# A transformer block on one NeuronCore: weight splits and background products placed differently at the attention entry and ahead of three norms

## The chip, the cores and the metric

The kernel runs on one core of a Trainium2 chip. The metric is the device time of one execution in microseconds (us), lower is better. Engines are named as the profile names them: PE is the matrix engine (PEld its weight loads), DVE the vector engine, ACT the scalar engine, POOL GpSimd, SP the engine that issues most DMAs.

## What is computed

One sequence of 256 tokens with 1024 channels goes through two blocks. The first has two layers, each a token mixer and a gated feed-forward net (FFN); the second is a state-space and pooling block with a mixture of experts. Each layer starts from an RMS norm whose result is scaled and shifted by vectors that come from a conditioning input (adaLN).

```python
def first_block(...):
    for i in range(DEPTH):
        mod = (silu_c @ ada_w[i] + ada_b[i])[:, None, :]
        sh1, sc1, g1, sh2, sc2, g2 = jnp.split(mod, N_MOD, axis=-1)
        h = modulate(rmsnorm(x, norm1_g[i]), sh1, sc1)
...
        if mixer == 0:
            yc, y = diff_attention(h, hc, ...)
        elif mixer == 1:
            yc, y = short_conv(h, hc, ...)
...
        x = x + g1 * y
        x = x + g2 * swiglu(modulate(rmsnorm(x, norm2_g[i]), sh2, sc2), ffn_w_in[i], ffn_w_out[i])
def second_block(...):
        u = modulate_2(rmsnorm_2(h, norm_mix_g[l]), sh1, sc1)
        proj = u @ w_in[l]
```

So the chain of stages is: attention, FFN 0, short convolution, FFN 1, the input product of the second block and its branches, experts.

## The kernel before

**Products.** Tokens lie along the free axis (T = 256), channels along the 128 partitions, so a 1024-channel activation is 8 tiles. A product in 32-bit precision is made of three matmuls (`mm3`, lines 280 to 282): high weight part by high activation, high by low, low by high. One output tile of 128 channels with 8 input tiles is therefore 24 matmuls.

**Weights.** A `Stream` brings them in 1 MB tiles (ring of 4). A unit is half a tile, 8 blocks of 128x128, so with 1024 input channels one output takes one unit. Each unit is split just ahead of its use: ACT copies the high part (`wh`, line 146), DVE subtracts to get the low part (`wl`, line 134), into a ring of 5 units. `take(n, ahead)` hands out blocks and first splits up to `ahead` units beyond the one taken; `more(n)` only splits. Both engines work strictly in the order in which the instructions were issued, so a split that is issued ahead of other work is done ahead of it.

**Background.** With each new unit, `take` also issues a share (`bg_pace`) of the adaLN sums: one weight tile by the conditioning row on DVE (`ada`, line 395), 128 in all. `hold` stops them.

**Attention.** A loop over the value products (4 steps) runs heads' scores and exponentials for the first three head halves; then a loop over 18 steps does, per step, on PE a transpose of the probabilities (`turn_p`, tile tp, copied to pT by ACT at line 801), the next scores (tile s), and the product with the values (`attend`, line 809, tile o); on DVE the maxima of the scores (line 722) and the difference of the two softmaxes (lines 737, 738); on ACT the exponentials (line 728).

**Residual.** `residual` (called after attention, after each FFN and after the convolution) makes the 8 output tiles (ps_r, or the first of them together: ps_wo, ps_so), adds each to x on DVE (line 910), squares it on ACT for the norm's mean square (`sumsq_step`, line 338) and, ahead of the three norms of class `Raw`, also splits the raw x into u (lines 930, 931).

**Norms ahead of which products run.** `Raw` covers the waiting time of a norm: the first products of the next stage are made from the un-normed u and are multiplied by the norm's rows later (`lift`). `Raw.run` does this with 3 outputs at the convolution's entry (raw1: ps_cu, ps_cu, ps_b), 4 at FFN 1 (raw3: ps_f) and 4 at the second block (raw2: ps_ssd, beside some small dt products). In it come in turn: one input tile's products of all outputs, the mean square on PE (ms, line 351), its inverse root on DVE (rs_v to rs_r), more products, the rows on PE (line 953), a copy of them (rows_s, line 956), the remaining products, and the norm itself: DVE scales x (na, line 379), ACT shifts it to hh (line 380), DVE makes the low part hl (line 383). After that all products use hh and hl. FFN 0's entry has the plain form, without products ahead (line 363).

Of the kernel before, what the change touches and what calls it, by code (L numbers as in the profile page):

```python
# [8 lines left out]
F32 = mybir.dt.float32  # L9
# [8 lines left out]
P = 128  # L18
T = 256
D = 1024  # L20
KD = 8
# [86 lines left out]
class Stream:  # L108
# [51 lines left out]
    def more(self, n, defer=False):  # L160

        self.fill(self.pos // 8 // 2 + self.ring)
        self.split_to(self.pos // 8 + n, defer)
# [74 lines left out]
class Builder:  # L238
# [93 lines left out]
    def sumsq_step(self, ms, xk, k, tag="rp_a", **kw):  # L332

        nc = self.nc
        sq = self.wk.tile([P, T], F32, tag=tag if k == 0 else "sq", name="sq", bufs=2)
        if k == 0:
            self.acc[tag] = sq
        nc.scalar.activation(sq, xk, AF.Square, **kw)  # L338
        if 0 < k < KD - 2:
            nc.gpsimd.tensor_tensor(self.acc[tag], self.acc[tag], sq, op=ALU.add)  # L340
        if k == KD - 2:
            self.acc[tag, 1] = sq
        if k == KD - 1:
            self.totals.append((ms, (self.acc[tag], self.acc[tag, 1], sq)))
# [80 lines left out]
def build(ctx, tc, ap):  # L425
    b = Builder(ctx, tc, ap)
# [319 lines left out]
    for n in range(4):  # L746
        pss = [b.ps.tile([P, 2, T], F32, tag="ps", name="ps_v") for _ in range(2)]
# [23 lines left out]
    b.bg_pace = 0.0  # L771
# [72 lines left out]
    for s in range(18):  # L844
# [6 lines left out]
        if s + 3 < 16:  # L851
            scores(s + 3)
        if s >= 4 and s % 2 == 0:
            head_turn((s - 4) // 2)
# [17 lines left out]
        if s < 13:  # L872
            st.ahead_splits()
        if s == 13:
            st.more(4)
# [10 lines left out]
    def residual(ktiles, xh, xl, gate, sums, done=(), raw=None):  # L886
# [10 lines left out]
        for n in range(KD):  # L897
            if n < len(done):
                ps = done[n]
            else:  # L900
                b.hold = raw is not None and n == KD - 1
# [6 lines left out]
                if raw and n == KD - 1:  # L908
                    st.more(4)
# [6 lines left out]
    class Raw:  # L916
# [16 lines left out]
        def steps(self, outs, more):  # L933
            w = st.take(KD * len(outs), 0)
            for k in range(KD):
                if more:
                    more(k)
                for i, o in enumerate(outs):
                    b.mm3(o[:, :T + 2], w[i * KD + k], self.H[:, k], self.L[:, k], k == 0, k == KD - 1)
                yield  # L940

        def run(self, rstd, outs, more=None):

            go = self.steps(outs, more)
            next(go)
            b.total()
            r = self.r = rstd()
            st.more(5 - len(outs))
            next(go)
            next(go)  # L950
# [180 lines left out]
    pss = [b.ps.tile([P, 2, T], F32, tag="ps", name="ps_so") for _ in range(2)]  # L1131
    so_out = together([pss[i // 2][:, i % 2] for i in range(4)], rH, rL)
# [1180 lines left out]
```

## Time and profile before

| | us |
|---|---|
| median of 3 runs | 1561.92 |
| lowest and highest run | 1558.98, 1562.48 |
| the profiled execution | 1554.01 |
| its span from first to last instruction | 1552.2 |
| PE busy | 1480.8 (95%) |
| DVE busy | 987.8 (64%) |
| ACT busy | 669.0 (43%) |
| PE clock over the span, share of full | 0.988 |

The profiled execution is 7.9 us shorter than the median. Times inside the trace count from the start of the span. Stages lie there as follows: attention's 18 steps from 155 to 217, FFN 0 from 236, the convolution's entry at 431, FFN 1's entry at 524, the second block's entry at 724, the experts from about 1000 on. A row with a bracket tells how long its engine was idle before and what ended that.

### The profile page before, as it was taken

The page shows a single profiled execution, that of the slowest core. Times are in us where ns is not written, and L with a number is a line of the kernel's source. Part 1 is how long each engine was busy: PE and PEld are TensorE (multiplying, and loading weights), DVE is VectorE, ACT ScalarE, POOL GpSimd, SP SyncE. Part 2 cuts the span into 40 slices and gives each one's busy share as a digit, 9 for nine tenths or more (in the row PEclk, how much of TensorE's full clock was granted, in tenths as well). Part 3 has the DMA queues.
Part 4 walks back from the last instruction along what each step waited for, and adds up shares of the span by engine and source line. Part 5 has one row for each costly group of instructions (what it writes and reads, how often), then busy time and mean ns, then how long its engine had stood idle before and what let it go on. Part 6 is the DMA issues. An engine that isn't in the chain of part 4 may idle for free. (4 is left out here: it accounts for less than half of the span.)

```text
span 1552.2 us, 28284 instructions
## 1 busy us (share of the span) xinstructions
PE 1480.8 (95%) x11184; PEld 1185.0 (76%) x11184; DVE 987.8 (64%) x1850; ACT 669.0 (43%) x1175; POOL 276.2 (18%) x439
## 2 busy tenths in 40 slices
PE   6999888999999999999899999999999999999996
PEld 5788578999999899999899998999634444444432
DVE  3698767888888789887888877465423333323332
ACT  3524554544455454454677765443322222222222
POOL 0170560000100100021067667001100000000000
PEclk9999999999999899999999999999999999999998
DMA  9678224987957569786444544667489999999995
GB/s 388 224 247 284 103 73 186 347 326 292 352 197 250 191 231 355 297 312 236 145 167 153 190 164 154 237 249 324 164 310 414 420 419 421 420 419 420 421 420 210
DMA packets 71429, 431.93 MB, mean 278 GB/s; under 512 B 8176, under 2 KB 8688, under 8 KB 28416
## 3 DMA queue, kind: packets, MB, share of 16 engines
q1 hardware_dynamic: 68656, 422.77, 71.0%
q0 software_dynamic: 1344, 4.80, 0.8%
q10 hardware_dynamic: 1296, 2.55, 0.5%
q8 instruction: 88, 1.44, 0.4%
q14 instruction: 45, 0.37, 0.1%
HBM read 429.01 MB, written 1.08 MB: 277 GB/s over the span
## 5 line engine op out<-in xcount | busy, mean ns | idle before, releaser
L134 DVE TENSOR_TENSOR wl<-st,wh 128x1024 fp32r<-128x1024 f32 x294 | 364.7, 1249 | 74.5 <-ACT wh L146 74.0
L146 ACT ACTIVATE wh<-st 128x1024 fp32r<-128x1024 f32 x294 | 306.2, 1055 | 113.2 <-PE ps_r L281 45.2
L280 PE MATMUL ps_f<-hh,wh 128*128 128x256 f32 x672 | 189.6, 282 | 2.5 <-ACT hh L380 2.1
L282 PE MATMUL ps_f<-hh,wl 128*128 128x256 f32 x672 | 189.5, 282 | 0.7 <-DVE wl L134 0.7
L281 PE MATMUL ps_f<-hl,wh 128*128 128x256 f32 x672 | 189.4, 282 | 0.1
L395 DVE SCALAR_TENSOR_TENSOR ada<-ada,crow 128x1024 f32<-128x1024 f32 x128 | 164.8, 1295 | 18.3 <-DMA ada<-in_ada 18.3
L340 POOL TENSOR_TENSOR sq<-sq 128x256 f32<-128x256 f32 x30 | 40.5, 1356 | 575.6 <-ACT sq L338 575.2
L280 PEld LDWEIGHTS ps_f<-hh,wh 128*128 128x128 f32 x672 | 127.6, 190 | 2.9 <-ACT hh L380 2.3
L282 PEld LDWEIGHTS ps_f<-hh,wl 128*128 128x128 f32 x672 | 127.5, 190 | 1.0 <-DVE wl L134 1.0
L281 PEld LDWEIGHTS ps_f<-hl,wh 128*128 128x128 f32 x672 | 127.6, 190 | 0.3 <-DVE hl L383 0.3
L280 PE MATMUL ps_ssd<-hh,wh 128*128 128x256 f32 x352 | 101.4, 288 | 0.0
L280 PE MATMUL ps_r<-gH,wh 128*128 128x256 f32 x352 | 98.7, 280 | 0.0
L281 PE MATMUL ps_r<-gL,wh 128*128 128x256 f32 x352 | 98.7, 280 | 0.0
L282 PE MATMUL ps_r<-gH,wl 128*128 128x256 f32 x352 | 98.7, 280 | 0.0
L282 PE MATMUL ps_ssd<-hh,wl 128*128 128x256 f32 x352 | 98.6, 280 | 0.0
L281 PE MATMUL ps_ssd<-hl,wh 128*128 128x256 f32 x352 | 98.6, 280 | 0.0
L1817 DVE TENSOR_SCALAR xb<-gtp,A,mod 128x256 f32<-128x256 f32 (+2 forms) x52 | 27.4, 526 | 111.5 <-ACT xb L1815 111.3
L1815 ACT ACTIVATE xb<-gtp,mod,A 128x256 f32<-128x256 f32 (+2 forms) x52 | 28.6, 551 | 118.6 <-PE gtp L1835 118.4
L1805 POOL TENSOR_TENSOR WG<-G,pwq 128x256 f32<-128x256 f32 (+2 forms) x24 | 14.1, 608 | 366.4 <-DVE G L1801 366.4
L274 ACT ACTIVATE oH<-wr 128x512 fp32r<-128x512 f32 (+2 forms) x53 | 33.4, 630 | 95.2 <-DVE wr L2093 82.6
L1835 PEld LDWEIGHTS gtp<-G,utH 128*128 128x128 f32 x208 | 39.2, 189 | 45.9 <-DVE xb L1817 19.7
L280 PEld LDWEIGHTS ps_ssd<-hh,wh 128*128 128x128 f32 x352 | 66.3, 188 | 1.0 <-issue 1.0
(616 smaller groups left out, 4156.0 us busy)
## 6 DMA issues: line engine op xcount, KB each, us to landing
st<-in_ws SPq DMA_DIRECT2D x151, 1024.0 KB, 6.0
ada<-in_ada SPq DMA_DIRECT2D x128, 512.0 KB, 5.0
w<-in_we SPq DMA_DIRECT2D x40, 1024.0 KB, 19.8
w_st<-in_we SPq DMA_DIRECT2D x40, 1024.0 KB, 19.8
w_y<-in_we SPq DMA_DIRECT2D x32, 1024.0 KB, 19.8
w_ut<-in_we SPq DMA_DIRECT2D x30, 1024.0 KB, 19.8
w_h<-in_we SPq DMA_DIRECT2D x21, 1024.0 KB, 19.8
x<-in_we SPq DMA_DIRECT2D x10, 1024.0 KB, 19.8
```

What stands on the lines that cost most here:

```text
L134: self.b.nc.vector.tensor_tensor(lo.rearrange("p a c -> p (a c)"), w, h.rearrange("p a c -> p (a c)"), op=ALU.subtract)
L146: nc.scalar.activation(h.rearrange("p a c -> p (a c)"), w, AF.Copy)
L274: self.nc.scalar.activation(h, src, AF.Copy)
L280: nc.tensor.matmul(out, lhsT=h[:, k], rhs=xh, start=start, stop=False, skip_group_check=True)
L281: nc.tensor.matmul(out, lhsT=h[:, k], rhs=xl, start=False, stop=False, skip_group_check=True)
L282: nc.tensor.matmul(out, lhsT=lo[:, k], rhs=xh, start=False, stop=stop, skip_group_check=True)
L340: nc.gpsimd.tensor_tensor(self.acc[tag], self.acc[tag], sq, op=ALU.add)
L395: self.nc.vector.scalar_tensor_tensor(junk, w, 1.0, crow, op0=ALU.mult, op1=ALU.mult, accum_out=dst[:, j:j + 1])
L1805: nc.gpsimd.tensor_tensor(cut(WG, tt), cut(G, tt), ws_[:, tt][:, :, None].to_broadcast([P, n, c]), op=ALU.mult)
L1815: nc.scalar.activation(out[:, k, :n], tp[:, i, :n], AF.Identity, scale=A, bias=B)
L1817: nc.vector.tensor_scalar(out[:, k, :n], tp[:, i, :n], A, B, op0=ALU.mult, op1=ALU.add)
L1835: nc.tensor.matmul(tp[:, i, :n], lhsT=hl_[:, tt, k * P:(k + 1) * P], rhs=G[:, tt, :n], start=(i == 0 and tt == 0 and hl_ is utH), stop=(tt ...
```

## The change

Five edits. The square of the last but one tile goes into another ring (`na`, 3 buffers), so that the last one finds a buffer. The adaLN sums stop one step earlier in the value loop. The two units of the output weights that were split at steps 13 and 14 of the attention loop are split at steps 0 and 2. In `residual`, the hold of the adaLN sums begins at the fifth output instead of the last after the convolution, and the split of units at the last output is gone. In `Raw`, the outputs are no longer made all together but the first two together and each other by itself, the mean square comes after three input tiles, the rows after all eight; the units of later outputs are taken, with up to three further units split, when their turn comes. The convolution's output product makes 2 instead of 4 outputs together.

```diff
 def sumsq_step(self, ms, xk, k, tag="rp_a", **kw):
-        sq = self.wk.tile([P, T], F32, tag=tag if k == 0 else "sq", name="sq", bufs=2)
+        kept = k == KD - 2
+        sq = self.wk.tile([P, T], F32, tag="na" if kept else "sq" if k else tag, name="sq", bufs=3 if kept else 2)
...
     for n in range(4):
+        if n == 3:
+            b.bg_pace = 0.0
...
-    b.bg_pace = 0.0
...
+        if s in (0, 2):
+            st.more(4 + s // 2)
...
-        if s < 13:
-            st.ahead_splits()
-        if s == 13:
-            st.more(4)
+        if 2 < s < 14:
+            st.more(5)
...
-                b.hold = raw is not None and n == KD - 1
+                b.hold = raw is not None and n >= (KD - 1 if ktiles > KD else 4)
...
-                if raw and n == KD - 1:
-                    st.more(4)
...
         def steps(self, outs, more):
-            w = st.take(KD * len(outs), 0)
-            for k in range(KD):
-                if more:
-                    more(k)
-                for i, o in enumerate(outs):
-                    b.mm3(o[:, :T + 2], w[i * KD + k], self.H[:, k], self.L[:, k], k == 0, k == KD - 1)
-                yield
+            for g in (outs[:2], *[[o] for o in outs[2:]]):
+                w = st.take(KD * len(g), 4 - len(g))
+                for k in range(KD):
+                    if more and g[0] is outs[0]:
+                        more(k)
+                    for i, o in enumerate(g):
+                        b.mm3(o[:, :T + 2], w[i * KD + k], self.H[:, k], self.L[:, k], k == 0, k == KD - 1)
+                    yield
...
-            next(go)
+            for _ in range(3):
+                next(go)
             b.total()
             r = self.r = rstd()
-            st.more(5 - len(outs))
-            next(go)
-            next(go)
+            for _ in range(KD - 3):
+                next(go)
...
-    pss = [b.ps.tile([P, 2, T], F32, tag="ps", name="ps_so") for _ in range(2)]
-    so_out = together([pss[i // 2][:, i % 2] for i in range(4)], rH, rL)
+    pss = [b.ps.tile([P, 2, T], F32, tag="ps", name="ps_so")]
+    so_out = together([pss[0][:, i] for i in range(2)], rH, rL)
```

Three places show what this moves. On DVE at the start of the attention loop, before: wl is a low weight part, ada an adaLN sum, smx the maxima of the scores of the fourth head half.

```order
L134 TENSOR_TENSOR wl<-st,wh 128x1024
L395 SCALAR_TENSOR_TENSOR ada_553,mod_92<-ada_553,crow 128x1024
L395 SCALAR_TENSOR_TENSOR ada_554,mod_92<-ada_554,crow 128x1024
L134 TENSOR_TENSOR wl<-st,wh 128x1024
L395 SCALAR_TENSOR_TENSOR ada_552,mod_92<-ada_552,crow 128x1024
L395 SCALAR_TENSOR_TENSOR ada_553,mod_92<-ada_553,crow 128x1024
L400 TENSOR_TENSOR mod_92<-mod_92,vecs 128x8
L722 TENSOR_REDUCE smx<-s 128x1 x2
L732 RECIPROCAL smx<-smx 128x2
```

The same place on DVE in the changed kernel:

```order
L134 TENSOR_TENSOR wl<-st,wh 128x1024 x2
L723 TENSOR_REDUCE smx<-s 128x1 x2
L134 TENSOR_TENSOR wl<-st,wh 128x1024
L733 RECIPROCAL smx<-smx 128x2
L738 TENSOR_SCALAR smx<-smx,lam 128x1
```

Four sums and an addition have left the queue ahead of the maxima, and one split of the output weights has come in behind them.

On ACT at the convolution's entry (raw1), before: rows_s is the copy of the norm's rows, hh the norm's result.

```order
L338 ACTIVATE sq<-x 128x256
L930 ACTIVATE u<-x,A_1_96 128x256
L146 ACTIVATE wh<-st 128x1024
L956 ACTIVATE rows_s<-rows 128x256
L380 ACTIVATE hh<-na,mod_93 128x256 x8
L146 ACTIVATE wh<-st 128x1024 x2
```

The same place on ACT in the changed kernel:

```order
L339 ACTIVATE sq<-x 128x256
L930 ACTIVATE u<-x,A_1_96 128x256
L146 ACTIVATE wh<-st 128x1024
L958 ACTIVATE rows_s<-rows 128x256
L146 ACTIVATE wh<-st 128x1024 x2
L381 ACTIVATE hh<-na,mod_93 128x256 x8
```

Two splits have moved from behind the norm's eight tiles to ahead of them. At raw3 and raw2 it is three.

On DVE at the same entry, before: rs_r is the last step of the inverse root, na and hl the two steps of the norm.

```order
L321 SCALAR_TENSOR_TENSOR rs_r<-rs_t,rs_r 128x1 x2
L134 TENSOR_TENSOR wl<-st,wh 128x1024
L379 SCALAR_TENSOR_TENSOR na<-x,A_1_96,rows_s 128x256 x3
L383 SCALAR_TENSOR_TENSOR hl<-na,mod_93,hh 128x256
L379 SCALAR_TENSOR_TENSOR na<-x,A_1_96,rows_s 128x256
```

The same place on DVE in the changed kernel:

```order
L321 SCALAR_TENSOR_TENSOR rs_r<-rs_t,rs_r 128x1 x2
L134 TENSOR_TENSOR wl<-st,wh 128x1024 x2
L380 SCALAR_TENSOR_TENSOR na<-x,A_1_96,rows_s 128x256 x3
L384 SCALAR_TENSOR_TENSOR hl<-na,mod_93,hh 128x256
L380 SCALAR_TENSOR_TENSOR na<-x,A_1_96,rows_s 128x256
```

The one split that stood there has moved ahead of the inverse root, and the two of ACT's list stand in its place, each behind its wh.

## Rows read from the trace of the kernel before

**Rows 1.** PE waits over the whole span: engine, line, releaser, total, times, longest us.

```profile
PE o L809 <- ACT pT L801: 9.0, 6, 4.0
...
PE ps_f L282 <- DVE wl L134: 3.9, 4, 1.8
```

**Rows 2.** Timeline of DVE at attention's entry: start us, duration us, instruction, idle before.

```profile
159.42 1.23 DVE L395 SCALAR_TENSOR_TENSOR ada<-ada,crow 128x1024 f32<-128x1024 f32 x1 [0.40 <-DMA ada<-in_ada]
...
160.77 1.28 DVE L722 TENSOR_REDUCE smx<-s 128x1 f32<-128x512 f32 x2
```

**Rows 3.** Timelines of ACT (second row) and PE over attention's first steps.

```profile
155.74 1.13 PE L719 MATMUL s<-kT,qT 64*128 64x512 f32 x4
...
161.49 0.69 ACT L728 ACTIVATE se<-s,smx 128x512 f32<-128x512 f32 x1 [4.99 <-DVE smx L722]
...
163.48 0.79 PE L809 MATMUL o<-v,pT 128*128 128x128 f32 x2 [4.03 <-ACT pT L801]
...
168.34 0.58 PE L809 MATMUL o<-v,pT 128*128 128x128 f32 x1
...
177.94 0.49 PE L809 MATMUL o<-v,pT 128*128 128x128 f32 x2 [0.79 <-ACT pT L801]
```

**Rows 4.** Costliest groups of the page: count | busy us, mean ns | idle before.

```profile
L134 DVE TENSOR_TENSOR wl<-st,wh 128x1024 fp32r<-128x1024 f32 x294 | 364.7, 1249 | 74.5 <-ACT wh L146 74.0
L146 ACT ACTIVATE wh<-st 128x1024 fp32r<-128x1024 f32 x294 | 306.2, 1055 | 113.2 <-PE ps_r L281 45.2
```

**Rows 5.** Timeline of DVE at FFN 0's entry.

```profile
236.27 1.22 DVE L395 SCALAR_TENSOR_TENSOR ada<-ada,crow 128x1024 f32<-128x1024 f32 x1
...
237.63 0.16 DVE L289 TENSOR_SCALAR rs_v<-ms 128x4 f32<-128x4 f32 x1
```

**Rows 6.** Timeline of PE at raw1: its first raw product, the last of the first output with hh.

```profile
430.71 0.28 PE L280 MATMUL ps_cu<-u,wh 128*128 128x258 f32 x1
...
443.83 0.28 PE L282 MATMUL ps_cu<-hh,wl 128*128 128x256 f32 x1
```

**Rows 7.** Timelines of PE, ACT and DVE around raw1's norm, and ACT's two splits.

```profile
435.29 0.39 PE L953 MATMUL rows<-csts,rs_r 128*128 128x128 f32 x2
...
435.94 0.38 ACT L956 ACTIVATE rows_s<-rows 128x256 f32<-128x256 f32 x1 [2.68 <-PE rows L953]
...
436.36 1.28 DVE L379 SCALAR_TENSOR_TENSOR na<-x,A,rows_s 128x256 f32<-128x256 f32 x3 [0.38 <-ACT rows_s L956]
...
442.13 1.27 DVE L383 SCALAR_TENSOR_TENSOR hl<-na,mod,hh 128x256 fp32r<-128x256 f32 x3
...
442.67 2.00 ACT L146 ACTIVATE wh<-st 128x1024 fp32r<-128x1024 f32 x2
```

**Rows 8.** Timelines of DVE (second row) and PE from raw3's start to FFN 1.

```profile
523.85 0.28 PE L280 MATMUL ps_f<-u,wh 128*128 128x258 f32 x1
...
530.68 0.48 DVE L910 SCALAR_TENSOR_TENSOR x<-ps_r,mod,x 128x256 f32<-128x256 f32 x1
...
548.58 0.28 PE L282 MATMUL ps_f<-hh,wl 128*128 128x256 f32 x1
...
550.54 0.39 PE L282 MATMUL ps_f<-hh,wl 128*128 128x256 f32 x1 [0.75 <-DVE wl L134]
```

**Rows 9.** Timelines of ACT (first row) and PE at raw2.

```profile
727.62 0.42 ACT L338 ACTIVATE sq<-x 128x256 f32<-128x256 f32 x1 [5.18 <-PE ms L351]
...
744.07 0.28 PE L282 MATMUL ps_ssd<-u,wl 128*128 128x258 f32 x1
...
746.89 0.28 PE L282 MATMUL ps_ssd<-hh,wl 128*128 128x256 f32 x1
```

**Rows 10.** Windows: length, busy PE, PEld, DVE, ACT, POOL, then PE clock, DMA share, GB/s.

```profile
160.00:165.00 5.00, 1.52 (x7) 1.52 (x8) 4.38 (x11) 3.08 (x8) 0.00 (x0) 0.70 0.90 268
...
244.00:248.00 4.00, 4.00 (x23) 4.00 (x23) 3.89 (x11) 2.69 (x5) 0.00 (x0) 0.59 0.00 0
...
932.00:936.00 4.00, 2.52 (x15) 1.05 (x14) 2.98 (x5) 1.56 (x3) 3.91 (x4) 1.00 0.13 14
```

## The prediction

> **What bounds the kernel now.** The first look goes to the busy shares: PE works for 95% of the span, so time can only come or go where PE waits, or where its clock is down. The second look is PE's list of waits: the probabilities copied by ACT in attention, 9.0 us in 6 waits with one of 4.0, and the low weight parts at FFN 1's entry, 3.9 us in 4 waits [rows 1]. Those are two of the places that the change touches; the other three (raw1, raw2, FFN 0's entry) are read from timelines, since there PE waits little and what counts is how much cover is left. The third look is the clock: 0.70 in the window of attention's entry, 0.59 at FFN 0's start, where 23 matmuls stand in 4 us [rows 10]; at full clock 24 of them take the 2.82 us from 744.07 to 746.89 [rows 9], 0.118 each, so 34 would fit.
>
> **Attention's entry.** Before, DVE has four adaLN sums ahead of the maxima of the fourth head half; the last starts at 159.42 after 0.40 of waiting for its DMA, and the maxima start at 160.77 [rows 2]. ACT's exponentials have waited 4.99 for them and start at 161.49, PE's second value product starts at 163.48, 4.03 late [rows 3]. Without the sums (about 1.2 each from start to start, 0.40 of waiting, 5.1 together) the maxima could begin at 155.7. The scores that they read start on PE at 155.74 and take 1.13 [rows 3], so they are complete about 156.9, and the first split of the output weights now stands ahead of the exponentials on ACT, one wh of 1.06 [rows 4]. So the exponentials start near 158 and the value product near 160.1, a gain of 3.3. The next product came 4.86 after it before [rows 3], in a window with the clock at 0.70 [rows 10]; with the second wl queued ahead of the combination it comes about 3.8 after, near 163.9: gain 4.4. From there the old pace holds, 9.60 for three steps [rows 3]. Bounds: 3.3 (only the first wait goes) to 5.1 (all that left the queue ahead of the maxima). I take **-4.4**. At the loop's end two wl and two wh are gone from steps 13 and 14. The end hangs on a chain through POOL, so I take **-0.3** of a possible 0 to -1.2 (one wl). The third wh of ACT or wl of DVE that the new place adds is in the numbers above.
>
> **FFN 0's entry.** The sums that left must be done somewhere. Two rather than one now stand between the last x and rs_v. Before, the one at 236.27 ends just ahead of rs_v at 237.63 [rows 5]; the second pushes rs_v by its 1.22, less the 0.14 and a little more that DVE idled between the two: **+1.0**, wholly on the path, since this entry has no products to cover it. The other sums go under FFN 0's dense products, where DVE has room; if it had none they would cost 1.2 each.
>
> **raw1.** Here the cover was just enough: raw products from 430.71, then hh products without a stop, the first such output ends at 443.83 [rows 6]. Between rows on PE at 435.29 and hl's end at 443.40 lie 0.65 to rows_s, 0.42 to na and 7.04 for the eight tiles [rows 7]. Before, rows came after 27 raw products (three tiles of three outputs) and the mean square; now they come after 48 (eight tiles of two), 21 x 0.118 = 2.5 later, at 437.8. The inverse root does not delay them: it had 18 products between mean square and rows and now has 30, 1.4 us more, for the one wl of 1.25 that is put ahead of it. rows_s at 438.4. Then ACT splits two units (2.00 for two [rows 7]), to 440.7, and DVE's second wl, of 1.25 and a handover behind the second wh, ends at 442.2. Only then na; hl ends 7.04 later at 449.2, and the first hh output at 449.4. PE's work up to there ends with the third raw output, 24 products behind rows, at 441. So 449.4 against 443.83: **+5.6**. Of it 2.5 is for rows that come later, 3.1 for the splits, of which nothing is hidden; what hid them before, the products with hh, now waits for them. The two wl that DVE had behind the norm are gone there, which keeps the rest in step. Bounds: +4.5 to +6.0.
>
> **raw3.** Here before it is DVE that lags: the last x is added at 530.68, although PE had begun the raw products at 523.85 and stood waiting for low parts; the first hh output ends at 548.58, and for the next three matmuls, to 550.54, it needs 1.96 instead of 0.36 [rows 8], waiting for a high and a low part. The cause is that four outputs made together deliver four x at once, and three splits and a sum come ahead of their u. With two together and six by themselves, x is 2.84 behind its predecessor, against 0.48 for x, as much for u and 1.25 for a wl of work per output on DVE: the last x comes at about 524.1. The mean square costs PE 1.4 (in raw1 4.58 from the first raw product to rows, less 27 x 0.118 [rows 6, 7]); with 48 products of the pairs rows come at 523.85 + 5.7 + 1.4 = 530.9, rows_s at 531.5, three wh end at 534.8, three wl at 536.5, hl at 543.5, the first hh output at 543.7. PE has the two single outputs till 537 and then starves. Gain 4.9, and 1.6 for the gaps behind, whose units are now split beforehand: **-6.5**, bounds -5.4 to -7.6.
>
> **raw2.** The last square no longer waits 5.18 for PE [rows 9], worth 0.6 of PE's time at the mean square. The raw work as a whole is the same and ended at 744.07; now it ends at 743.5, and the 48 products of the single outputs (5.7) and rows (0.4) are its last part, so rows come at 737.4, rows_s at 738.0. Three wh end at 741.3, three wl at 742.6, hl at 749.6, the first hh output at 749.8 against 746.89 [rows 9]: +2.9. DVE is then 7 late with two wl less to do before the second block's short convolution, which may cost a little more: **+3.0**, bounds +2.2 to +3.8.
>
> The SP queue keeps its order of loads; other stages keep their instructions. **Sum: -4.4 - 0.3 + 1.0 + 5.6 - 6.5 + 3.0 = -1.6.**
>
> **The clock.** In raw1, raw3 and raw2 PE is now fed three matmuls each 0.92 us (an eighth of hl's 7.04, with the pauses) for some 6.5 us, in raw1 after 1.6 us of nothing. The trace has both answers: a stretch with waits in it at full clock, 2.4 GHz (the last window of [rows 10]), and the fall to 1.2 GHz at attention's entry, where PE had idled for 4.03 (the first window there, [rows 3, 10]). raw1, with its pause, is nearer to the second, the other two nearer to the first. A fall costs what PE loses after the dense products are back: 34 - 23 = 11 matmuls of 0.118 in 4 us, 1.3 [rows 10], up to twice that if the low clock stays twice as long; I take 2.1. With one fall, at raw1, the sum is **+0.5**, and that is the forecast.
>
> The Trainium skill, TensorE: Matmul & The Clock Gate, section "HAM oscillation — how this bites in real kernels", says that a TensorE that waits between bursts falls back to its lower clock time after time. The two falls in rows 10 agree with it; the last window there, waits at full clock, shows that not each wait does it. Taken strictly, all three places would pay, which is rival A.
>
> **Rivals.**
> A, slower: the clock falls at all three places ahead of a norm. -1.6 + 3 x 2.1 = +4.7, so 1566.6. It decides from the second fall on. For it speaks that each place is thinly fed for over 6 us; against it the full clock in the window at 932.
> B, slower: the entry gains nothing, because the early wh and wl of the output weights stand in the chain of maxima, exponentials and combinations, as two of 1.06 and two of 1.25 can [rows 4]. Then a gain of 4.7 is down to about 1: +0.5 + 3.7 = +4.2, so 1566.1. Against it: ACT idled 4.99 there.
> C, faster: PE's clock holds at all three, and raw3 and the entry give their upper bounds. -1.6 - 1.1 - 0.7 = -3.4, with the smaller loss of +4.5 at raw1 -4.5: about 1557.5. For it: PE is never wholly idle for long at raw3 and raw2.
> That the change does not do what it says is excluded by the order of the instructions.
>
> **How the numbers follow.** The profiled execution took 1554.01, the median is 1561.92, 7.9 more; the sum is made in the profiled one and carried to the median as it stands: 1561.92 + 0.5 = 1562.4 (1554.5 beside the profiled). About 0.2%, 3.1 us, can be told from no change. Chances: forecast (sum between -3 and +3, none or one or two falls) 0.45, A 0.20, B 0.10, C 0.25. That makes faster 0.25, same 0.45, slower 0.30. The forecast's own range is 1559 to 1565; to hold 8 in 10 it reaches down to C with the entry's and raw3's upper ends, -6 (1556), and up to A with a part of B, +6.5 (1568.5).
>
> **What would show it.** Right: the second value product near 160 and no window under full clock about 165; x's last addition before raw3 at most 1 us behind PE; at raw1 rows_s followed by two wh on ACT and a hole of 2 us on PE, then hl-bound products; PE's list with hh from hl (line 384) in place of wl. Wrong: na starting right behind rows_s (the splits then cost nothing, and raw1 gives only +2.5), the old gap at attention's second value product, or a late stage that gives back what was won, which I have put at nothing because weights stream in an unchanged order behind it.

## The result and the profile after

The changed kernel takes 1571.64 us in the median of its 8 runs (1568.14 to 1574.97), the kernel before 1558.49 in 8 runs beside them (1552.47 to 1562.48). The ratio is 1.009 with a 95% interval of 1.007 to 1.0109: slower by 13 us, where +0.5 was forecast. That is above the predicted range, which ended at +6.5, and beyond rival A's +4.7. (The median of 1561.92 given above is that of the first three of the eight runs of before.)

The page of the changed kernel, its span and its busy times:

```profile
span 1569.3 us, 28279 instructions
...
PE 1492.4 (95%) x11184; PEld 1196.0 (76%) x11184; DVE 987.1 (63%) x1850; ACT 669.3 (43%) x1175; POOL 272.9 (17%) x439
...
PEclk9999999999999999998899999999999999999999
```

PE is busy for 11.6 us more than before, on the same products. About half of it is low clock: the mean granted clock is 0.984 for 0.988 before, which makes some 13 us more at half speed and so some 6 us of work (an estimate). The two eights are slices of 39 us, from 706 to 785. What is new in PE's list of waits (engine, line, releaser, total, times, longest):

```profile
PE o L811 <- ACT pT L803: 7.0, 8, 1.8
PE cb L1345 <- ACT sb L1285: 5.9, 1, 5.9
PE ps_p L280 <- DVE wb L970: 5.6, 1, 5.6
...
PE ps_cu L280 <- ACT hh L381: 1.9, 1, 1.9
```

The two waits that the change aimed at did shrink: the probabilities no longer hold one wait of 4.0, and the low weight parts of FFN 1's entry (3.9 in [rows 1]) are off the list. Two waits of over 5 us stand in their place, both at the second block's entry, raw2.

The two traces are cut at the same instructions in each. The first value product starts at 156.80 before and 160.27 after, FFN 0's first product at 242.05 and 241.26, the first dt product of raw2 at 724.61 and 722.73, the first `cbm` of the second block on DVE at 763.66 and 782.79. The first raw products of raw1 and raw3 are 430.71 and 523.85 before [rows 6, 8], and after:

```profile
429.10 0.28 PE L280 MATMUL ps_cu<-u,wh 128*128 128x258 f32 x1
...
527.87 0.28 PE L280 MATMUL ps_f<-u,wh 128*128 128x258 f32 x1
```

| stretch | before, us | after, us | difference | predicted |
|---|---|---|---|---|
| start to first value product | 156.80 | 160.27 | +3.5 | 0 |
| to FFN 0's first product | 85.25 | 80.99 | -4.3 | -4.4 - 0.3 + 1.0 = -3.7 |
| to raw1 | 188.66 | 187.84 | -0.8 | 0 |
| to raw3 | 93.14 | 98.77 | +5.6 | +5.6, and +2.1 of clock |
| to raw2 | 200.76 | 194.86 | -5.9 | -6.5 |
| to the first cbm | 39.05 | 60.06 | **+21.0** | **+3.0** |
| to the end | 788.54 | 786.51 | -2.0 | 0 |

The differences add up to 17.1 us, the difference of the two spans; the medians differ by 13.1. The +3.5 at the start is not work of the change. PE waits alike for its first load (9.29 us in both), but then takes twice as long for the same eight products, before and after:

```profile
20.57 1.99 PE L625 MATMUL ps_q<-full,st 128*128 128x256 f32 x8 [1.55 <-ACT full L532]
20.99 3.78 PE L626 MATMUL ps_q<-full,st 128*128 128x256 f32 x8 [1.56 <-ACT full L533]
```

The granted clock of the profile is 1.00 in both, so why is not shown. Kernels without the change start late too: the kernel before, profiled once more, starts its first value product at 158.63. All terms of the sum but one are within a microsecond or so. Nearly the whole miss is one stretch of 40 us, raw2.

**What stands in it.** DVE at raw2, after (start, duration, instruction, idle before and what ended it):

```profile
743.12 3.50 DVE L134 TENSOR_TENSOR wl<-st,wh 128x1024 fp32r<-128x1024 f32 x3 [11.36 <-ACT wh L146]
...
752.31 1.27 DVE L384 SCALAR_TENSOR_TENSOR hl<-na,mod,hh 128x256 fp32r<-128x256 f32 x3
753.50 1.22 DVE L396 SCALAR_TENSOR_TENSOR ada<-ada,crow 128x1024 f32<-128x1024 f32 x1
...
754.64 1.22 DVE L396 SCALAR_TENSOR_TENSOR ada<-ada,crow 128x1024 f32<-128x1024 f32 x1
...
759.06 1.22 DVE L396 SCALAR_TENSOR_TENSOR ada<-ada,crow 128x1024 f32<-128x1024 f32 x1 [3.19 <-DMA ada<-in_ada]
...
762.05 1.23 DVE L396 SCALAR_TENSOR_TENSOR ada<-ada,crow 128x1024 f32<-128x1024 f32 x1 [1.76 <-DMA ada<-in_ada]
...
763.48 0.42 DVE L969 TENSOR_TENSOR lift<-ps_ssd,rows_s 128x256 f32<-128x256 f32 x1
...
782.79 0.55 DVE L1348 TENSOR_TENSOR cbm<-cb,mask 128x384 f32<-128x384 f32 x1
```

Four adaLN sums stand between the norm's last low part and the first `lift`, for 10 us, of which 4.95 are waits for their own loads. They are the rest of the 128: the second block needs them there, so the program issues all that are still left right behind raw2's norm. Before, none was left. The entry now stops the sums one step earlier and `hold` keeps them from four outputs instead of one, while `bg_pace`, the share of sums per weight unit, is a fixed number (0.7), so nothing takes them up elsewhere. Counted in the two traces, the change takes three sums from ahead of FFN 0's first product (30 for 33) and two from raw1 to raw3 (8 for 10); one more is done from raw3 to raw2 (42 for 41), and four are left.

PE in the same stretch, after:

```profile
726.99 2.94 PE L352 MATMUL ms<-ones,sq 128*128 128x2 f32 x24
729.79 0.40 PE L1200 MATMUL ps_dt<-wd,u 128*128 128x64 f32 x1
...
740.66 1.06 PE L955 MATMUL rows<-csts,rs_r 128*128 128x128 f32 x4
...
764.11 0.55 PE L280 MATMUL ps_p<-hh,wh 128*128 128x256 f32 x1 [5.64 <-DVE wb L970]
...
780.00 0.79 PE L1345 MATMUL cb<-sb 128*128 128x256 f32 x1 [5.92 <-ACT sb L1285]
```

Windows of it (length, busy PE, PEld, DVE, ACT, POOL, then PE clock, DMA share, GB/s), after:

```profile
725.00:730.00 5.00, 4.94 (x40) 4.67 (x39) 1.71 (x5) 0.31 (x2) 0.00 (x0) 0.94 0.02 8
730.00:735.00 5.00, 5.00 (x25) 5.00 (x25) 1.69 (x14) 0.00 (x0) 0.00 (x0) 0.50 0.00 0
735.00:740.00 5.00, 5.00 (x24) 5.00 (x24) 0.00 (x0) 0.00 (x0) 0.00 (x0) 0.50 0.00 0
740.00:745.00 5.00, 5.00 (x33) 5.00 (x32) 1.88 (x2) 3.23 (x4) 0.00 (x0) 0.70 0.00 0
```

The clock is at 1.2 GHz for the ten microseconds ahead of rows, although PE never stops there: 24 or 25 matmuls in 5 us. In the trace of before the same stretch ran at 2.4 GHz:

```profile
730.00:735.00 5.00, 5.00 (x42) 4.79 (x42) 3.36 (x19) 0.80 (x2) 0.00 (x0) 1.00 0.02 3
```

So raw2 can be cut once more, from its first dt product on: to rows on PE (734.31 before, 740.66 after), to the first lift (743.30 before, 763.48 after), to the first cbm.

| part of raw2 | before | after | difference | of which |
|---|---|---|---|---|
| first dt product to rows | 9.70 | 17.93 | +8.2 | 3.1 predicted for the order; 5.1 left for the clock |
| rows to first lift | 8.99 | 22.82 | +13.8 | 10.0 sums; 3.85 splits ahead of the norm |
| first lift to first cbm | 20.36 | 19.31 | -1.05 | a wait of DVE for ACT's wh, 0.88 before, is gone; low parts are seven in both |

### The profile page after: what moved, and what is told of

It reads as the page before. It is cut to its first block, busy times and chain, and to the rows that moved or that the text cites. A ratio compares the mean times of both kernels' runs of the same rounds, so it can differ in the third digit from the quotient of the medians.

```text
span 1569.3 us, 28279 instructions
## 1 busy us (share of the span) xinstructions
PE 1492.4 (95%) x11184; PEld 1196.0 (76%) x11184; DVE 987.1 (63%) x1850; ACT 669.3 (43%) x1175; POOL 272.9 (17%) x439
## 5 line engine op out<-in xcount | busy, mean ns | idle before, releaser
L1837 PEld LDWEIGHTS gtp<-G,utH 128*128 128x128 f32 x208 | 39.2, 188 | 45.9 <-DVE xb L1819 19.7
L281 PEld LDWEIGHTS ps_ssd<-hl,wh 128*128 128x128 f32 x352 | 67.2, 191 | 2.7 <-DVE hl L384 2.7
```

Of the source, the lines that this page charges most:

```text
L281: nc.tensor.matmul(out, lhsT=h[:, k], rhs=xl, start=False, stop=False, skip_group_check=True)
L1837: nc.tensor.matmul(tp[:, i, :n], lhsT=hl_[:, tt, k * P:(k + 1) * P], rhs=G[:, tt, :n], start=(i == 0 and tt == 0 and hl_ is utH), stop=(tt ...
```

## The experiments

The same cuts were read in the trace of every kernel that ran; the table gathers what the sections below use. "Left" is the number of sums that the program issues behind raw2's norm.

| kernel | left | median, us | ratio [95%] | raw1 to raw3 | raw3 to raw2 | dt to rows | rows to lift | lift to cbm |
|---|---|---|---|---|---|---|---|---|
| before | 0 | 1558.49 | 1 | 93.1 | 200.8 | 9.7 | 9.0 | 20.4 |
| before, second trace | 0 | one run, 1566.39 | | 92.4 | 201.0 | 14.3 | 9.1 | 20.4 |
| after | 4 | 1571.64 | 1.009 [1.007, 1.0109] | 98.8 | 194.9 | 17.9 | 22.8 | 19.3 |
| a_pace | 0 | 1565.01 | 1.0047 [1.0025, 1.0068] | 100.3 | 194.8 | 18.0 | 12.9 | 19.7 |
| a_late | 4 | 1565.4 | 1.0044 [1.0021, 1.0067] | 95.7 | 193.4 | 21.3 | 18.2 | 19.3 |
| a_both | 0 | 1559.99 | 1.0001 [0.9978, 1.0024] | 95.6 | 193.0 | 23.6 | 8.6 | 19.7 |
| a_warm | 4 | 1574.26 | 1.0094 [1.0063, 1.0125] | 99.4 | 194.5 | 15.6 | 21.6 | 19.3 |
| b_entry | 2 | 1556.06 | 0.9989 [0.9967, 1.0012] | 92.4 | 201.5 | 13.7 | 11.0 | 19.3 |
| b_so | 1 | 1549.46 | 0.9941 [0.9921, 0.996] | 92.4 | 192.0 | 13.6 | 9.9 | 20.2 |
| b_rawna | 0 | 1570.18 | 1.0088 [1.0059, 1.0117] | 99.9 | 200.9 | 15.9 | 12.5 | 19.7 |
| b_flush4 | 4 | 1565.62 | 1.0054 [1.0037, 1.0071] | 92.4 | 199.3 | 12.4 | 16.9 | 19.3 |
| b_best | 0 | 1547.07 | 0.9923 [0.9897, 0.9949] | 93.1 | 193.6 | 12.6 | 10.1 | 20.3 |
| b_best_again | 0 | 1545.08 | 0.9918 [0.9889, 0.9947] | 93.1 | 192.9 | 9.0 | 9.0 | 20.3 |
| b_bestwarm | 0 | 1548.97 | 0.9937 [0.9913, 0.9961] | 93.1 | 192.4 | 14.5 | 10.0 | 20.3 |
| b_pair2 | 0 | 1554.78 | 0.998 [0.9963, 0.9997] | 93.1 | 192.9 | 21.8 | 8.6 | 19.7 |
| b_pair13 | 0 | 1549.89 | 0.9947 [0.9925, 0.9969] | 95.6 | 193.0 | 14.5 | 9.2 | 20.3 |

### Are the sums left over on the path?

Two kernels ask it from both sides. a_pace is the changed kernel with a higher share, so that all sums are done before raw2:

```diff
-    b.bg_pace = 0.7
+    b.bg_pace = 0.78
     b.need(("L1", 2))
```

> The changed kernel with one number raised: the share of adaLN sums per weight unit from the convolution's output product on is 0.78 instead of 0.70, so that no sum is left when the second block's norm is done. In the changed kernel's trace four sums stand on DVE between the last hl (753.5) and the lift of the raw products (763.5), two of them waiting 3.19 and 1.76 us for their loads. Theory 1, those four sums are the larger part of the 13 us loss: the lift and all behind it come 9.9 us earlier, the 5.6 us wait of PE for wb (line 970) is gone, and the run takes 9 to 11 us less than the changed kernel (about 1561 to 1563, near before). Theory 2, the order of the raw products and the low clock there make the loss: 0 to 2 us less than the changed kernel (1570 to 1572).

b_flush4 is the kernel before with a lower share at the same line (0.62), so that just four sums are left at raw2:

> The kernel before with one number lowered: the share of sums per weight unit from the convolution's output product on is 0.62 instead of 0.70, which leaves exactly four sums to be done at the second block between hl and the lift, as in the changed kernel; nothing else moves on PE or ACT. Theory 1 (four sums there cost their time and the waits for two loads, on the path): 7 to 11 us slower than before. Theory 2 (most of it is hidden by products with hh): 0 to 3 us slower.

a_pace gave back 6.6 us, less than the 9 to 11 expected of the sums, though far more than nothing. In its trace PE's wait for `wb` is gone and the one for cb is down:

```profile
PE cb L1345 <- ACT sb L1285: 3.5, 1, 3.5
```

There raw2 is 9.5 us shorter (rows to lift 12.9 for 22.8), as expected; 3 of it did not reach the run time. Where they went is not settled: raw1 to raw3 is 1.5 longer in this trace, which would fit sums that now stand there, but single traces differ by as much for other reasons. b_flush4 is 7.0 us slower than before, at the low end of what was expected. In its trace the sums stand where they stand in after, and two wait for their loads:

```profile
745.49 1.27 DVE L383 SCALAR_TENSOR_TENSOR hl<-na,mod,hh 128x256 fp32r<-128x256 f32 x3
...
751.46 1.23 DVE L395 SCALAR_TENSOR_TENSOR ada<-ada,crow 128x1024 f32<-128x1024 f32 x1 [2.41 <-DMA ada<-in_ada]
...
753.80 1.23 DVE L395 SCALAR_TENSOR_TENSOR ada<-ada,crow 128x1024 f32<-128x1024 f32 x1 [1.11 <-DMA ada<-in_ada]
...
755.23 0.42 DVE L967 TENSOR_TENSOR lift<-ps_ssd,rows_s 128x256 f32<-128x256 f32 x1
```

So four sums left over cost 6.6 to 7.0 us, in either kernel.

### Each part alone

The change is six edits (the list above calls them five). b_entry is the kernel before with the attention entry's edits only (the earlier stop of the sums, the earlier output weights):

> The kernel before with the two edits of the attention entry alone (sums stop one step earlier, output weights split at steps 0 and 2). Attention and FFN 0's entry gain 3.7 us together, as in the changed kernel's trace. The sums that left attention run over at the other end: two are left at the second block and stand there between hl and the lift. Theory 1, these cost 2.3 us of DVE and up to 5 us of waiting for their loads: the whole is between 2 us faster and 4 us slower than before. Theory 2, sums left over cost nothing since PE has other work: 3 to 4 us faster.

It gained 2.4 us, which the measurement can't tell from nothing, and so not the one theory from the other. Two sums are left over in it, and rows to lift is 2.0 longer than before: some of the attention's 4 us is lost there.

b_so has the longer hold and the convolution's two outputs together, on the kernel before:

```diff
-                b.hold = raw is not None and n == KD - 1
+                b.hold = raw is not None and n >= (KD - 1 if ktiles > KD else 4)
...
-    pss = [b.ps.tile([P, 2, T], F32, tag="ps", name="ps_so") for _ in range(2)]
+    pss = [b.ps.tile([P, 2, T], F32, tag="ps", name="ps_so")]
```

> The kernel before with two edits alone: the convolution's output product makes two outputs together and six one by one, and the sums are held from the fifth output on. The raw products of FFN 1 stay four together. Theory 1, DVE's lag behind PE is what cost time there: the last x is added within 1 us of PE's end (6.9 us late before), FFN 1's first hh output comes about 6 us earlier, and one sum left at the second block costs 1 to 3: 3 to 6 us faster than before. Theory 2, the gain in the changed kernel came from making the raw products two by two: here 0 to 2 us faster.

It gained 9.0 us, more than expected: raw3 to raw2 takes 192.0 for 200.8 before. All of raw3's gain comes from these two edits (which of them, no run tells); none of the kernels with these two edits takes over 195 in that stretch, whatever order `Raw` has, and none without them under 199.

b_rawna has the new order in `Raw` alone (with it goes the split of units at the last output), with the square's other ring, without which the last square would wait for PE's mean square, which in the new order stands behind products whose weight split is queued behind that square on ACT:

> The kernel before with the new order of the raw products alone (pairs, then one by one; mean square after three input tiles; later units split ahead of the norm) and the square's other buffer, which that order needs. No sum is left over at the second block. Theory 1 (order, splits and clock cost by themselves): raw1 +5 to +8, raw2 +9 to +12 of which 6 is low clock during pairs and dt products, raw3 +2 to +5 since DVE still lags there: 15 to 22 us slower than before. Theory 2 (the loss needs the sums left over): 3 to 7 us slower.

It lost 11.5 us. That lies between what the two theories said. The trace puts it at raw1 to raw3 (99.9 for 93.1) and at raw2 (48.1 in all for 39.1 or, with the second trace of before, 43.7); at raw3 nothing is won.

The three add up to -2.4 - 9.0 + 11.5 = +0.1, and the change measured +13.1. The parts are not independent: alone they leave 2, 1 and 0 sums, together 4. A chain of kernels that follow adds up better. From before to b_best (all that wins, no sum left) it is -11.6, from there to a_both (the new order, no split ahead of the norm) +12.9, to a_pace (splits ahead of the norm) +5.0, to the changed kernel (four sums left) +6.6, together +12.9. So the order with its early splits costs 17.9 beside the other edits and 11.5 alone; where the other 6 come from was not taken apart.

### The splits ahead of the norm

a_late is the changed kernel with no unit split between rows and the norm:

```diff
-            for g in (outs[:2], *[[o] for o in outs[2:]]):
-                w = st.take(KD * len(g), 4 - len(g))
+            for j, g in enumerate((outs[:2], *[[o] for o in outs[2:]])):
+                w = st.take(KD * len(g), 3 - j)
```

> The changed kernel, but the raw products' later outputs split no unit between the norm's rows and the norm: one unit more is split with the pair, the rest after the norm as in the kernel before. The four sums at the second block stay. Theory 1, a split that stands ahead of the norm delays it by its full time: the first hh output comes about 3 us earlier at the convolution's entry and about 4 us earlier at FFN 1 and at the second block, less about 1.6 us at FFN 1 where PE again waits for units split after the norm: 7 to 10 us less than the changed kernel in all, 1562 to 1565. Theory 2, the splits only change places and PE waits for them behind the norm instead: 0 to 2 us less.

It gained 6.2 us. raw1 to raw3 is 3.1 shorter, as much as the prediction had put on the two splits there; but the low clock that after has at raw1 is gone too, so the 3.1 holds both (from 443 to 449, after and a_late):

```profile
443.00:449.00 6.00, 5.92 (x22) 5.12 (x23) 5.55 (x17) 3.15 (x6) 0.00 (x0) 0.50 0.28 117
443.00:449.00 6.00, 6.00 (x53) 6.00 (x52) 5.51 (x16) 2.42 (x4) 0.00 (x0) 1.00 0.53 171
```

At raw2 rows to lift is 4.6 shorter, but a low part that the norm's products need is now queued behind the four sums:

```profile
PE ps_ssd L282 <- DVE wl L134: 10.6, 1, 10.6
```

a_both takes both edits, pace and late splits:

> The changed kernel with both mends: no sum left over, and no unit split between rows and norm. If the two add up (6.6 and 6.2 measured apart): about 1559. With less overlap, since in the kernel with late splits alone PE waited 10.6 us for one low part behind the four sums: 1553 to 1557. If they mend the same wait: 1562 to 1565.

1559.99 us, level with before, as if the two added up. What the entry and the two outputs together win, the new order in `Raw` still eats.

### The order itself

b_best is the kernel before with all edits but the new order in `Raw` (entry, hold, two outputs together, the square's ring) and a pace of 0.78:

> The changed kernel's other edits on the kernel before, without the new order of the raw products: attention entry, output weights, hold, two outputs together at the convolution's output, the square's buffer, and the share of sums raised to 0.78 so that none is left at the second block. Theory 1 (gains of the entry and of FFN 1's entry are real and independent, -2.4 and -9.0 as measured apart, and one to two sums less at the second block): 1543 to 1548, 10 to 15 us faster than before. Theory 2 (the two measured gains share a cause, or the added sums are missed elsewhere): 1549 to 1553.

It takes 1547.07 us, 0.8% under before and within the range of theory 1, and 1545.08 when run again beside the next two:

> The kernel with the good edits and the old order of raw products once more, as the base for the next two: 1547 +- 3.

Against a_both the order costs 12.9 us. b_pair2 and b_pair13 put it back into b_best (with late splits), at raw2 alone and at raw1 and raw3 alone:

> That base with the new order (pairs, mean square after three tiles, rows after eight, no split ahead of the norm, no sum left over) at the second block alone. Theory 1 (the order costs there, because the mean square of two norms pulls PE's clock down and rows now wait for five more tiles of pairs and small dt products at 1.2 GHz, 2.15 us each instead of 1.15): 6 to 10 us slower than the base, 1553 to 1557. Theory 2 (each of the three places pays about alike for rows that come 2.5 us later): 2 to 4 us slower.

> The base with the new order at the convolution's entry and at FFN 1 alone. Theory 1: 2.5 us at the convolution's entry and about 1 at FFN 1, 2 to 5 us slower than the base. Theory 2 (alike at all places): 6 to 9 us slower.

b_pair2 is 9.7 us slower than b_best_again, b_pair13 4.8 (8.3 and 3.4 against the ten runs of b_best and b_best_again together). So some two thirds of the order's price is raw2's. There the two traces differ in dt to rows, 21.8 for 9.0 (12.6 in b_best, whose trace has a low clock there). b_pair2 has the low clock from 719.3 on, 4.3 us behind its first dt product:

```profile
720.00:725.00 5.00, 5.00 (x26) 5.00 (x25) 0.35 (x2) 0.00 (x0) 0.00 (x0) 0.50 0.45 190
...
730.00:735.00 5.00, 5.00 (x26) 5.00 (x24) 0.00 (x0) 0.00 (x0) 0.00 (x0) 0.50 0.00 0
```

Rows come after eight tiles of two outputs, 48 products beside 32 small dt products, where they came after three tiles of four, 36 beside 12, and a product of 256 columns takes 0.21 us for 0.12 when the clock is down.

Not all of it is the order, though. With late splits one more wh stands on ACT ahead of a copy (dtc) that PE needs, so PE waits, and the clock is down before the mean square begins:

```profile
716.43 1.99 ACT L146 ACTIVATE wh<-st 128x1024 fp32r<-128x1024 f32 x2
718.58 0.43 PE L1230 MATMUL ps_c<-dtc,ones 1*128 1x64 f32 x2 [1.00 <-ACT dtc L1227]
720.90 5.11 PE L352 MATMUL ms<-ones,sq 128*128 128x2 f32 x24
```

In a_late PE waits 1.01 there, in a_both 2.20, and the three have the longest dt to rows, 21.3 to 23.6. With the splits ahead of the norm (after, a_pace, b_rawna) PE does not wait there, and it is 15.9 to 18.0. Which part of the order (pairs, mean square after three tiles, rows after eight) costs most was not run apart. At raw1 and raw3 b_pair13 shows 2.5 in raw1 to raw3 (95.6 for 93.1) and nothing at raw3; 2.5 is the prediction's price for rows that come 21 products later. The run time's 4.8 is more than that; its rest is open.

### The clock at raw2

Is the low clock the cause, rather than a companion? a_warm is the changed kernel with 24 extra matmuls among the mean square's at raw2, whose result is not used, to keep PE at work there; b_bestwarm is b_best with 12:

```diff
+                    if self.warm:
+                        o, l, r = self.warm
+                        self.nc.tensor.matmul(o, lhsT=l, rhs=r, start=True, stop=True, skip_group_check=True)
```

> The changed kernel with 24 extra matmuls (256 columns each, into an unused part of a tile, result not read) put between the mean-square products at the second block's entry, two behind each. They cost PE 24 x 0.118 = 2.8 us. In the changed kernel's trace the clock falls to 1.2 GHz behind those products, at 729, and stays there until 742, through the pairs and the small dt products. Theory 1 (the low clock there costs some 6 us): the clock holds at 2.4 GHz, the raw phase is 3 us shorter on balance, and the run 2 to 4 us faster than the changed kernel, 1568 to 1570. Theory 2 (what follows waits for DVE anyway, so the clock there is hidden): 0 to 3 us slower, 1571.6 to 1574.5.

> The kernel with the good edits and the old order of raw products (1547.07), with 12 extra matmuls of 256 columns put between the mean-square products at the second block's entry, 1.4 us of PE. Theory 1 (the clock falls there in most runs of the old order too, and costs about 4): 1 to 3 us faster than that kernel. Theory 2 (it is hidden, or 12 are too few): 0 to 2 us slower.

In a_warm's trace the clock held: the five steps behind the mean square take 5.8 us for 10.9 in after. But the mean square itself takes 5.5 for 2.8, so rows come only 2.3 sooner, raw2 is 3.6 shorter, and the run time is no better (1574.26). PE then waits for DVE again:

```profile
PE ps_p L281 <- DVE wb L975: 6.3, 1, 6.3
```

b_bestwarm gains nothing either, and in its trace the clock fell all the same, at 722.7, at the end of the mean square. Neither shows a way to win the clock back, and what the fall costs in run time is not shown. a_warm does give the size of a fall in the trace: less the 2.7 of the extra matmuls, dt to rows would be 12.9 at full clock, 3.2 more than before, for 17.9 at the low one.

The kernel before was also profiled a second time:

> The kernel before, unchanged, for one more trace. The trace shown had PE at 2.4 GHz through the second block's entry and its first products early (155.15 for the first transpose). If those were luck of one execution, this trace shows the clock at 1.2 GHz for some 10 us from about 727 on and a start 2 to 3 us later; if they belong to this kernel, it shows neither.

Its run took 1566.39, 12.4 more than the profiled execution of the first trace and more than any other run of before (1564.07 at most), and the clock is down at raw2 there:

```profile
735.00:740.00 5.00, 5.00 (x25) 5.00 (x25) 3.29 (x17) 1.82 (x4) 0.00 (x0) 0.50 0.00 0
740.00:745.00 5.00, 5.00 (x23) 4.66 (x23) 0.52 (x3) 0.00 (x0) 0.00 (x0) 0.50 0.01 3
```

Without extra matmuls, dt to rows with the old order takes 9.0 and 9.7 in two traces and 12.4 to 14.5 in six. So the fall is no work of the change: the trace from which the prediction was made is one of those without it. With the new order the clock falls in six of six, and it takes 15.9 to 23.6.

## Why the prediction failed

**Attention, FFN 0's entry: right.** -3.7 predicted, -4.3 measured. Over all traces this stretch takes 81.0 to 83.5 with the entry's edits and 84.1 to 86.2 without. The second value product starts at 163.09, not near 160, because this trace started late; from the first value product it comes after 2.8 us for 6.7 before [rows 3]. The sums are gone from behind the scores and ACT no longer waits 4.99 but for a DVE that has just found the maxima:

```profile
160.37 1.29 DVE L723 TENSOR_REDUCE smx<-s 128x1 f32<-128x512 f32 x2 [1.32 <-PE s L720]
...
161.10 0.69 ACT L729 ACTIVATE se<-s,smx 128x512 f32<-128x512 f32 x1 [0.18 <-DVE smx L723]
```

**raw1: right.** The steps stand as told: rows_s, two wh, then the second wl, only then na, and PE's hole of 1.89 (ACT, DVE and PE in turn):

```profile
436.80 0.39 ACT L958 ACTIVATE rows_s<-rows 128x256 f32<-128x256 f32 x1 [5.15 <-PE rows L955]
...
437.08 2.01 ACT L146 ACTIVATE wh<-st 128x1024 fp32r<-128x1024 f32 x2
...
438.17 2.36 DVE L134 TENSOR_TENSOR wl<-st,wh 128x1024 fp32r<-128x1024 f32 x2 [3.76 <-ACT wh L146]
440.45 1.27 DVE L380 SCALAR_TENSOR_TENSOR na<-x,A,rows_s 128x256 f32<-128x256 f32 x3
...
441.52 0.38 PE L280 MATMUL ps_cu<-hh,wh 128*128 128x256 f32 x1 [1.89 <-ACT hh L381]
```

Of the 5.6, b_pair13 confirms 2.5 for late rows, and a_late has 3.1 for the splits together with the clock, which did fall there, from 442 to 449, as forecast. At the first product of ps_b with hh (446.77 before, 451.84 after) the difference was 6.7, at raw3 it is 5.6, so not all of the 2.1 on top lasted. The four traces with splits ahead of the norm take 98.8 to 100.3 here, +5.6 to +7.1; the prediction had +5.6 and, with the fall, +7.7. (An eighth of 7.04 is 0.88, not the 0.92 at which the prediction has PE fed; on PE the step is 0.92 all the same, as from 444.00 to 444.92.)

**raw3: right in size (-5.9 for -6.5); the cause leaves out the clock.** The last x now follows PE closely, for 6.83 behind raw3's first product [rows 8]:

```profile
528.07 0.48 DVE L910 SCALAR_TENSOR_TENSOR x<-ps_r,mod,x 128x256 f32<-128x256 f32 x1 [0.67 <-PE ps_r L282]
```

The runs add that the two outputs together and the hold bring it (b_so, 8.7 in this stretch), and that the new order takes little of it: nothing with late splits (193.0 in b_pair13 for 192.9), 1.5 to 1.8 with the splits ahead of the norm. Before, PE not only waited for DVE there: behind the waits its clock was down, which it is not in b_so:

```profile
532.00:537.00 5.00, 5.00 (x25) 5.00 (x25) 3.19 (x15) 1.02 (x2) 0.00 (x0) 0.50 0.78 309
531.00:536.00 5.00, 5.00 (x44) 5.00 (x43) 3.90 (x17) 1.51 (x5) 0.00 (x0) 1.00 0.71 285
```

All five traces without these two edits have this low clock at raw3, the others none or a third of it. From the start of the mean square to rows, where PE waits in neither, before takes 7.05 us (531.20 to 538.25) and b_so 4.22 (529.34 to 533.56), so at least 2.8 of the 8.7 is clock, of which the prediction has nothing at raw3.

**raw2: wrong, +21.0 for +3.0.** Three steps failed.

First, "The other sums go under FFN 0's dense products, where DVE has room; if it had none they would cost 1.2 each." Whether DVE had room or not, nothing sends the sums there: 44 are done from FFN 0's first product to raw1 in every trace. They are issued by a fixed share per unit, and what has not been issued by raw2 is issued there. Two more, held between raw1 and raw3 by the longer `hold`, were not counted at all. The order of the instructions alone, four rows of line 396 between the last hl and the first lift, would have told it. The price was also too low: with their loads they cost 10.0 us in the trace, 2.5 each, not 1.2, and 6.6 to 7.0 in the run time.

Second, "+3.0" was read from the wrong engine. The prediction has DVE "7 late" and takes 3.0, the lateness of PE's first hh output. But from lift to cbm the time is 19.3 to 20.4 in every trace, however late the lift is, and PE waits 2.4 for cb even before. DVE and ACT set the pace there (DVE waits for 1.2 of the 20.4 before), so the 7 count (3.1 for the order, 3.2 by a_warm, and 3.85 for the splits), less 1.05. Nor has DVE "two wl less to do" there: it makes seven between lift and cbm in every trace. The 1.05 is mostly a wait for ACT's wh that is gone. That is 3 more.

Third, the clock. A fall was put at 2.1 and at raw1, where it came, and looked for where the norm's tiles feed PE in drops. At raw2 it came earlier, at the end of the mean square, and there the products that rows wait for run at half speed: 5.1 us. The trace of before, without a fall at raw2, hid that this place has one in most traces; against the median of before, only a part of the 5.1 is the change's.

3.0 + 10.0 + 3 + 5.1 is the 21 of this stretch. By medians the change costs 13.1, since before has its own falls and the sums cost about 7 there; how much of it is the clock's is not shown, for a_warm, where the clock held, is no faster. Told by the chain of kernels: the gains were put at -4.4 - 0.3 + 1.0 - 6.5 = -10.2 and came as -11.6; the new order with its splits was put at +5.6 + 3.0 = +8.6, and 2.1 for the clock, and came as 17.9; the sums were put at nothing and came as 6.6.

The rivals had neither the sums nor the wrong engine. Rival A's falls came in part: in after the clock is down at raw1, shortly at raw3 (0.51 from 545 to 548.5) and at raw2, but raw1 and raw3 come out near the sum without them, and at raw2 the long fall lies ahead of the norm. The warning that closes the prediction named "a late stage that gives back what was won, which I have put at nothing because weights stream in an unchanged order behind it": it was looked for in the weights, and it was in the sums.

## What to carry to other kernels

Background work that is taken from one place has to be followed to the place where the program will force it: count in the order of instructions what is still left ahead of the first use, and choose the share anew with each change of holds (0.7 to 0.78 was worth 6.6 us here). At a stage's entry, read the lateness on the engine that sets the pace behind it, here DVE with lift and convolution, not on PE, which had cover. Work that others wait for, such as a norm's rows, should come after as few products as cover allows, since every product ahead of it costs nearly twice as much when the clock falls; and edits that win apart (two outputs together with the longer hold, 9 us) should be measured apart from one that loses.

## What the runs showed of the hardware that was not expected

Two traces of the same kernel before differ by 12.4 us (1552.2 and 1564.6 in span), 4.6 of it by the clock in dt to rows at raw2. The profile shows both:

```profile
core 0: 1564.6 us, clock 0.982
```

against 0.988 in the first. The table of stretches against one trace is therefore only good to a few microseconds a stretch, and medians decide.

A mean square of 24 matmuls of two columns counts as busy for 2.94 us in the profile, PE is 4.94 of 5.00 busy in its window, and yet in after the clock falls at its end and stays at 1.2 GHz for more than ten microseconds in which PE is busy without a stop. The Trainium skill, TensorE: Matmul & The Clock Gate, section "HAM oscillation — how this bites in real kernels", describes the fall for a TensorE that waits between bursts; here PE did not wait, nor in a_pace and b_rawna. In a_late, a_both and b_pair2 it had waited 1.0 to 2.2 us, and the clock fell ahead of the mean square. In before and b_best_again the same mean square was followed by no fall; with 24 larger matmuls among its own (a_warm) the clock held, with 12 (b_bestwarm) it fell, one trace each. What decides is not shown. That a low clock then lasts under full load agrees with [rows 10], where FFN 0's first products run at 0.59.

A sum that is not covered costs up to twice its instruction: 1.22 us on DVE, 2.5 with the waits of 3.19 and 1.76 for loads that were not started early enough. In each of the four traces with four sums left the first two do not wait and the last two do (1.11 to 3.19); the two of b_entry do not wait. The kernel keeps two tiles for these loads.
